# Attention probabilities of 14 of 16 heads turned on VectorE and through DRAM instead of on TensorE

## The chip, the cores and the metric

The kernel runs on 1 core of one Trainium2 chip. The metric is the device time of one execution, in microseconds (us). Engines are named as in the profile: PE is TensorE (PEld its weight loads), DVE is VectorE, ACT is ScalarE, POOL is GpSimd, SP is SyncE, which issues nearly all DMA transfers.

## What is computed

Two layers of a bidirectional encoder over 256 tokens of width 2048, in float32. Each layer projects the normalized input, runs three groups of attention heads side by side, gates them and projects back:

```
for l in range(DEPTH):                                   # 2
    proj = rmsnorm(x, norm_g[l]) @ w_in[l]               # 2048 columns to 5824
    ya = swa_attention(...)     # 8 heads, window |t-s| <= 128, sink logit, ALiBi
    yb = mla_attention(...)     # 4 heads, low-rank q and kv, rotary part
    yc = diff_attention(...)    # 4 heads, two softmax maps: a0 - lam * a1
    y = concat([ya * silu(a_g), yb * silu(b_g), yc * silu(c_g)])
    x = x + y @ w_out[l]
return rmsnorm(x, final_norm)
```

Every head makes a 256 x 256 map of probabilities p[q, k] by softmax over the keys, and then `out = p @ v`.

## The kernel before

All matrix products are done as three (or, stacked, two) products of halves: a float32 value is split into a rounded part `hi` and a rest `lo`, both of the type float32r. Weights come in pieces of 512 KB (line 150, tile `raw`, 4 buffers, issued by SP), are split by ACT into `whi` (line 176) and by DVE into `wlo` (line 177), 3 buffers each, and are used by PE. The list `pieces` sets the order: for each layer the wide projection (line 408), values of the C heads, up-projections of the B heads, gates, q and k of the C heads, then keys, queries and gates of the A heads (line 970 on), and 32 pieces of the output projection (line 834). Per piece of a transposed projection (`proj_t`, line 425) PE does 8 products with `whi` (line 437, 512 columns) and 8 with `wlo` (line 442, 256 columns).

The loop at line 1043 walks the pieces. `ahead` (line 984) puts loads up to four pieces and splits up to two pieces ahead into the program. `clock` counts pieces; `later(n, fn)` puts the work of a head n pieces on. Within an engine the instructions run in the order in which a list scheduler put them; PE follows the written order (`in_order`, line 76). SP issues its transfers in one row too: one that waits holds up all that stand behind it.

A head of group A or B goes like this. `scores` (lines 577 and 607): PE makes S = q k into PSUM, DVE adds the bias, DVE takes the maximum (line 540), ACT the exponential and its sum (line 542), DVE the reciprocal `rr` and the multiplication by it (lines 589 and 617, two halves of 128 x 256). The result is `sb`, queries on partitions, keys along the row. Three pieces later `transpose_p` (line 546): PE turns it in four 128 x 128 transposes into the PSUM tile `PT` (line 550), ACT and DVE split that into `pth` and `ptl` (line 181 and 183, through `halves`). Two pieces after that, `pv` (line 556): six products into `O`, and `put_y` (line 562) gates the result into `yhi`, `ylo`. A head of group C makes two maps one piece apart, `difference` (line 647) scales one on DVE (line 651) and subtracts (line 652), and the transposes follow five pieces after the first scores.

A map thus passes PE, DVE, ACT, DVE, PE, ACT and DVE, and PE again.

Of the kernel before, what the change touches and what calls it, by code (L numbers as in the profile page):

```python
# [61 lines left out]
def trunk(ctx, tc, x, positions, w_in, swa_sink, mla_w_uq, mla_w_ukv, diff_lambda, w_out, final_norm,  # L62
# [4 lines left out]
    const = pool("const")  # L67
    keep = pool("keep")
    wts = pool("wts")
    work = pool("work")  # L70
    small = pool("small", 4)
    acc = pool("acc", 4, space=bass.MemoryType.PSUM)
    att = pool("att", 4, space=bass.MemoryType.PSUM)

# [459 lines left out]
    def softmax(S_ps, sb, w, name):  # L534
# [8 lines left out]
        nc.vector.reciprocal(rr, sm)  # L543
        return rr

    def transpose_p(sb, name):
        ps = att.tile([P, NT, S], F32, tag="att", name=f"PT{name}")
        for kt in range(NT):
            for t in range(NT):
                nc.tensor.transpose(ps[:, kt, t * P:(t + 1) * P], sb[:, t, kt * P:(kt + 1) * P], ident)  # L550
        hi = work.tile([P, NT, S], F32R, tag="pth", bufs=2, name=f"pth{name}")
        lo = work.tile([P, NT, S], F32R, tag="ptl", bufs=2, name=f"ptl{name}")
        halves(hi, lo, ps)
        return hi, lo

    def pv(pt, v, d0, name):
        o = att.tile([P, S], F32, tag="att", name=f"O{name}")
        for kt in range(NT):
            mm3(o, v[0][:, kt, d0:d0 + P], v[1][:, kt, d0:d0 + P], pt[0][:, kt, :], pt[1][:, kt, :], kt == 0, kt == NT - 1)
        return o  # L560

    def put_y(L, e, o, gate):
# [5 lines left out]
        nc.vector.tensor_tensor(lo, y, hi.bitcast(F32), ALU.subtract)  # L568
        L.y[e] = (hi, lo)

    LAG_T, LAG_V = 3, 5

    def head_a(L, h):
        name = f"A{L.l}_{h}"
        st = {}

        def scores():
            ps = att.tile([P, NT, S], F32, tag="att", name=f"S{name}")
            (qh, ql), (kh, kl) = L.qa.pop(h), L.ka[h // (A_HEADS // A_KV)]
            for t in range(NT):  # L580
                ts = slice(t * P, (t + 1) * P)
                mm3(ps[:, t, :], qh[:, ts], ql[:, ts], kh, kl, True, True)
            sb = work.tile([P, NT, S + 1], F32, tag="sb", bufs=3, name=f"sb{name}")
            nc.vector.scalar_tensor_tensor(sb[:, :, :S], dist_a, -(2.0 ** -(h + 1)), ps, ALU.mult, ALU.add)
            i = L.l * A_HEADS + h
            nc.vector.tensor_copy(sb[:, :, S:S + 1], late["sink"][:, i:i + 1].unsqueeze(1).broadcast_to([P, NT, 1]))
            rr = softmax(None, sb, S + 1, name)
            for t in range(NT):
                nc.vector.tensor_scalar(sb[:, t, :S], sb[:, t, :S], rr[:, t:t + 1], None, ALU.mult)
            st["sb"] = sb  # L590

        def trans():
            st["pt"] = transpose_p(st["sb"], name)

        def out_():
            o = pv(st["pt"], L.va, (h // (A_HEADS // A_KV)) * P, name)
            put_y(L, h, o, L.ga.pop(h))

        scores()
        later(LAG_T, trans)  # L600
        later(LAG_V, out_)

    def head_b(L, h):
        name = f"B{L.l}_{h}"
        st = {}

        def scores():
            ps = att.tile([P, NT, S], F32, tag="att", name=f"S{name}")
            (qh, ql), (kh, kl) = L.qb.pop(h), L.kb.pop(h)
            for t in range(NT):  # L610
                ts = slice(t * P, (t + 1) * P)
                mm3(ps[:, t, :], qh[:, ts], ql[:, ts], kh, kl, True, False)
                mm_stacked(ps[:, t, :], L.qr[h // 2][h % 2], L.kr, ts, False, True)
            sb = work.tile([P, NT, S + 1], F32, tag="sb", bufs=3, name=f"sb{name}")
            rr = softmax(ps, sb, S, name)
            for t in range(NT):
                nc.vector.tensor_scalar(sb[:, t, :S], sb[:, t, :S], rr[:, t:t + 1], None, ALU.mult)
            st["sb"] = sb

        def trans():  # L620
            st["pt"] = transpose_p(st["sb"], name)

        def out_():
            o = pv(st["pt"], L.vb, h * P, name)
            put_y(L, A_HEADS + h, o, L.gb.pop(h))

        scores()
        later(LAG_T, trans)
        later(LAG_V, out_)

    def head_c(L, h):
        name = f"C{L.l}_{h}"
        st = {}

        sbs, rrs = [], []
        (q, k) = L.qc.pop(h), L.kc.pop(h)

        def scores(c):
            ps = att.tile([P, NT, S], F32, tag="att", name=f"S{name}_{c}")
            for t in range(NT):  # L640
                mm_stacked(ps[:, t, :], q[c], k[c], slice(t * P, (t + 1) * P), True, True)
            sb = work.tile([P, NT, S + 1], F32, tag="sb", bufs=3, name=f"sb{name}_{c}")
            nc.vector.scalar_tensor_tensor(sb[:, :, :S], dist, -(2.0 ** (-2.0 * (h + 1))), ps, ALU.mult, ALU.add)
            rrs.append(softmax(None, sb, S, f"{name}_{c}"))
            sbs.append(sb)

        def difference():
            lr = small.tile([P, NT], F32, tag="lr", name=f"lr{name}")
            nc.vector.tensor_scalar(lr, rrs[1], lam[:, L.l:L.l + 1], None, ALU.mult)
            for t in range(NT):  # L650
                nc.vector.tensor_scalar(sbs[1][:, t, :S], sbs[1][:, t, :S], lr[:, t:t + 1], None, ALU.mult)
                nc.vector.scalar_tensor_tensor(sbs[0][:, t, :S], sbs[0][:, t, :S], rrs[0][:, t:t + 1], sbs[1][:, t, :S], ALU.mult, ALU.subtract)
            st["sb"] = sbs[0]

        def trans():
            st["pt"] = transpose_p(st["sb"], name)

        def out_():
            o = pv(st["pt"], L.vc, h * P, name)
            sq = work.tile([P, S], F32, tag="ge", bufs=2, name=f"sq{name}")  # L660
            nc.scalar.activation(sq, o, AF.Square)
            hi = work.tile([P, S], F32R, tag="kf", bufs=2, name=f"sqh{name}")
            lo = work.tile([P, S], F32R, tag="kf", bufs=2, name=f"sql{name}")
# [17 lines left out]
        later(LAG_T + 2, trans)  # L681
        later(LAG_V + 3, out_)


    def evac_latent(L, which, t, ps):
        n = QR if which == 0 else KVR
        cn = L.cn[which, t] = work.tile([P, n], F32, tag=("pth", "ptl")[t], bufs=2, name=f"cn{L.l}_{which}_{t}")
# [5 lines left out]
        nc.vector.tensor_scalar(cn, ps[:, :n], rn, None, ALU.mult)  # L693
        if which == 0:
            if t == 0:
                L.krow = small.tile([P, NT, RD], F32, tag="krow", bufs=1, name=f"krow{L.l}")
            nc.vector.tensor_scalar(L.krow[:, t, :], ps[:, QR:QR + RD], r, None, ALU.mult)

    def latent_transpose(L, which):
# [182 lines left out]
    def load_final(L):  # L882
        L.fss = small.tile([P, NT, 5], F32, tag="fss", bufs=1, name="fss")
        L.gf = []
        for j in range(4):
            gf = work.tile([P, 512], F32, tag=("pth", "ptl")[j % 2], bufs=2, name=f"gf{j}")
# [42 lines left out]
    def build(L):  # L929
# [40 lines left out]
        for p in range(4):  # L970
            proj_t(L, w, AQ + 256 * p, lambda f, ps, p=p: evac_qk(L, L.qa, 2 * p + f, ps, P ** -0.5, "q"))
            proj_t(L, w, AG + 256 * p, lambda f, ps, p=p: evac_gate(L, L.ga, 2 * p + f, ps))
            task_piece(lambda p=p: (later(0, lambda: head_a(L, 2 * p)), later(1, lambda: head_a(L, 2 * p + 1))))
        for j in range(4):
            out_chunk(L, j)

# [112 lines left out]
```

## Time and profile before

| | us |
|---|---|
| median of 3 runs (797.11 to 797.41) | 797.26 |
| the profiled execution, whole | 797.44 |
| its span, first to last instruction | 795.1 |
| outside the span | 2.3 |
| PE busy | 785.3 |
| DVE busy | 619.9 |
| ACT busy | 490.1 |

An engine's row says how long it was busy. Matmuls are pipelined, so a PE that is busy throughout need not be at its peak; but when it never waits, each thing taken off it shortens the span. DMA moved 142 MB, and the packets of SP's queue took 58.5% of the time of the 16 DMA engines.

### The profile page before, as it was taken

How to read it: one execution, taken by the hardware profiler on the slowest of the kernel's cores; microseconds unless marked ns; L12 is line 12 of the kernel's file. 1: busy time of each engine (PE TensorE's matmuls, PEld its weight loads, DVE VectorE, ACT ScalarE, POOL GpSimd, SP SyncE). 2: the span in 40 equal slices, each digit the busy share in tenths (PEclk: the TensorE clock that was granted, in tenths of full speed). 3: DMA queues.
4: the chain of work that ended last, by engine and by line, in shares of the span. 5: the costliest groups of instructions: out<-in, count | busy, mean ns of one | idle time of the engine just before them, and what ended most of it. 6: DMA issues, size and time to landing. Idle time of an engine off the chain costs nothing.

```text
span 795.1 us, 12140 instructions
## 1 busy us (share of the span) xinstructions
PE 785.3 (99%) x4384; PEld 687.5 (86%) x4384; DVE 619.9 (78%) x1150; ACT 490.1 (62%) x920; POOL 32.6 (4%) x45
## 2 busy tenths in 40 slices
PE   9999999999999999999999999999999999999995
PEld 8888998888888888888888899988888888888885
DVE  6669997999988798655564878889998987875554
ACT  6668576767776566554454656667776766564442
POOL 4600000000000000000000000000000000002110
PEclk9999999999999999999999999999999999999998
DMA  9965665664665654555556666556565555557652
GB/s 321 364 180 155 185 176 158 161 184 145 172 167 155 169 174 154 165 188 183 189 181 187 179 170 194 147 144 184 142 196 165 158 158 160 164 170 230 198 165 106
DMA packets 113898, 141.99 MB, mean 179 GB/s; under 512 B 8240, under 2 KB 87344, under 8 KB 113840
## 3 DMA queue, kind: packets, MB, share of 16 engines
q1 hardware_dynamic: 113232, 139.69, 58.5%
q0 software_dynamic: 320, 1.05, 0.5%
q8 instruction: 34, 0.56, 0.3%
q10 hardware_dynamic: 288, 0.49, 0.2%
q14 instruction: 24, 0.20, 0.1%
HBM read 139.12 MB, written 2.10 MB: 178 GB/s over the span
## 4 chain that ended last, share of the span: by engine, by line
PE 98%; DVE 1%; DMA 1%; ACT 0%; issue 0%; ACTq 0%; DVEq 0%
PE pt L437 32%; PE pt L442 16%; PE po L386 7%; PE po L387 7%; PE po L389 7%; PE pw L389 4%; PE pw L386 3%; PE pw L387 3%; PE pa L389 2%; PE pa L386 2%; PE pa L387 2%; PE PTA L550 1%; DMA raw<-in_w_wide 1%; PE SA L305 0%; PE SC L496 0%; PE SA L307 0%
## 5 line engine op out<-in xcount | busy, mean ns | idle before, releaser
L177 DVE TENSOR_TENSOR wlo<-raw,whi 128x1024 fp32r<-128x1024 f32 (+1 forms) x257 | 313.5, 1222 | 132.8 <-ACT whi L176 131.2
L176 ACT ACTIVATE whi<-raw 128x1024 fp32r<-128x1024 f32 (+1 forms) x257 | 268.8, 1047 | 169.5 <-PE po L387 57.7
L437 PE MATMUL pt<-h,whi 128*128 128x512 f32 x1088 | 280.5, 395 | 0.0
L437 PEld LDWEIGHTS pt<-h,whi 128*128 128x128 f32 x1088 | 192.8, 188 | 32.5
L442 PEld LDWEIGHTS pt<-h,wlo 128*128 128x128 f32 x1088 | 152.8, 190 | 13.9
L442 PE MATMUL pt<-h,wlo 128*128 128x256 f32 x1088 | 156.9, 282 | 0.0
L386 PE MATMUL po<-whi,yhi 128*128 128x512 f32 (+1 forms) x262 | 101.3, 388 | 0.5 <-DVE x L901 0.5
L387 PE MATMUL po<-whi,ylo 128*128 128x512 f32 (+1 forms) x262 | 100.6, 385 | 0.0
L389 PE MATMUL po<-wlo,yhi 128*128 128x512 f32 (+1 forms) x262 | 70.7, 384 | 0.0
L386 PEld LDWEIGHTS po<-whi,yhi 128*128 128x128 f32 x262 | 49.2, 188 | 10.1 <-DVE x L901 0.7
L387 PEld LDWEIGHTS po<-whi,ylo 128*128 128x128 f32 x262 | 49.2, 188 | 9.4
L389 PEld LDWEIGHTS po<-wlo,yhi 128*128 128x128 f32 x262 | 48.8, 188 | 9.8
L386 PE MATMUL pw<-whi,h 128*128 128x448 f32 (+2 forms) x130 | 49.1, 379 | 0.4 <-ACT whi L168 0.4
L387 PE MATMUL pw<-whi,h 128*128 128x448 f32 (+2 forms) x130 | 48.9, 377 | 0.0
L389 PE MATMUL pw<-wlo,h 128*128 128x448 f32 (+2 forms) x130 | 33.0, 377 | 0.0
L567 ACT ACTIVATE yhi<-y 128x256 fp32r<-128x256 f32 x32 | 13.3, 416 | 30.5 <-DVE y L564 30.5
L887 POOL DMA_DIRECT2D gf<-in_final_norm x4 | 2.4, 598 | 681.1 <-PE OA L307 681.1
L386 PEld LDWEIGHTS pw<-whi,h 128*128 128x128 f32 x130 | 24.5, 188 | 4.2 <-ACT whi L168 0.5
L387 PEld LDWEIGHTS pw<-whi,h 128*128 128x128 f32 x130 | 24.4, 188 | 3.6
L389 PEld LDWEIGHTS pw<-wlo,h 128*128 128x128 f32 x130 | 24.1, 188 | 3.7
L386 PE MATMUL pa<-whi,h 128*128 128x512 f32 x64 | 25.3, 396 | 0.0
L387 PE MATMUL pa<-whi,h 128*128 128x512 f32 x64 | 25.1, 393 | 0.0
(337 smaller groups left out, 1053.2 us busy)
## 6 DMA issues: line engine op xcount, KB each, us to landing
raw<-in_w_in SPq DMA_DIRECT2D x152, 512.0 KB, 3.8
raw<-in_w_out SPq DMA_DIRECT2D x64, 512.0 KB, 4.3
raw<-in_w_wide SPq DMA_DIRECT2D x31, 480.0 KB, 4.0
raw<-in_mla_w_uq SPq DMA_DIRECT2D x18, 128.0 KB, 3.2
x<-in_x SPq DMA_DIRECT2D x4, 512.0 KB, 6.8
raw<-in_mla_w_ukv SPq DMA_DIRECT2D x8, 256.0 KB, 3.6
xt<-in_x_t SPq DMA_DIRECT2D x15, 128.0 KB, 5.4
out<-x SPq DMA_DIRECT2D x2, 768.0 KB, 3.3
```

Source lines behind the costliest of these rows:

```text
L176: nc.scalar.activation(p["hi"], raw, AF.Copy)
L177: nc.vector.tensor_tensor(p["lo"], raw, p["hi"].bitcast(F32), ALU.subtract)
L386: nc.tensor.matmul(ps, lhi, rhi, start=first, stop=False, skip_group_check=part)
L387: nc.tensor.matmul(ps, llo, rhi, start=False, stop=False, skip_group_check=part)
L389: nc.tensor.matmul(ps, lhi, rlo, start=False, stop=last, skip_group_check=part)
L437: nc.tensor.matmul(st["ps"][f], p["hi"][:, kk, f * P:(f + 1) * P], L.hh[k], start=k == 0, stop=False)
L442: nc.tensor.matmul(st["ps"][f][:, S:], p["lo"][:, kk, f * P:(f + 1) * P], L.h[k][0], start=False, stop=k == NK - 1)
L550: nc.tensor.transpose(ps[:, kt, t * P:(t + 1) * P], sb[:, t, kt * P:(kt + 1) * P], ident)
L567: nc.scalar.activation(hi, y, AF.Copy)
L887: nc.gpsimd.dma_start(gf, final_norm[j * 512:(j + 1) * 512].unsqueeze(0).partition_broadcast(P).rearrange("p a c -> p (a c)"))
```

## The change

In 14 of the 16 heads of each layer (all but the A heads 6 and 7, whose flag `by_pe` keeps the old way) PE transposes nothing. Instead:

- `turn_p`: two DVE instructions per head turn `sb` in squares of 32 x 32, 128 x 256 float32 each, directly behind the softmax, into a tile `T` whose row holds, for each of 4 blocks j of keys, all that goes to the partitions of block j: 512 bytes. T lies in the buffers `cTh` and `cTl`, one each, by turns.
- `spill_p`: SP writes T to a DRAM tile (256 KB, 2 KB a partition), two pieces after the softmax was written down; for C heads two pieces after `difference`.
- `fetch_p`: one piece later, SP reads it back in 4 transfers of 64 KB, one for each 32 partitions, in runs of 512 bytes, so that the squares lie in their places, in a tile `R` (tag `ptl`, now 3 buffers).
- `split_p`: three pieces after that ACT makes `hi` from R and DVE leaves R - hi in R itself; both are read from SBUF, where before they were read from PSUM.
- `pv` comes two pieces after that, so eight pieces after the scores where it was five. It reads hi and R in runs of 32 columns, with other runs between them, where it read rows of 256.
- The multiplication by `rr` of the B heads and by `lr` of the C heads goes from DVE to ACT.
- To find room, `small` has 3 buffers in place of 4 and two small tiles (`krow`, `krt`) use other tiles' buffers.

```
+    def turn_p(sb, name):
+        T = work.tile([P, P // Q, NT, NT, Q], F32, tag=("cTh", "cTl")[n_turned[0] % 2], bufs=1, name=f"T{name}")
+        n_turned[0] += 1
+        for t in range(NT):
+            nc.vector.transpose(T[:, :, :, t, :].rearrange("p j k b -> p k j b"),
+                                sb[:, t, :S].rearrange("p (k j b) -> p k j b", k=NT, b=Q))
+        return T
+    def spill_p(T, name):
+        dram = spill.tile([P, P // Q, NT * NT * Q], F32, tag="spill", name=f"D{name}")
+        nc.sync.dma_start(dram, T.rearrange("p j k t b -> p j (k t b)"))
+        return dram
+    def fetch_p(dram, name):
+        R = work.tile([P, P // Q, NT, NT, Q], F32R, tag="ptl", bufs=3, name=f"R{name}")
+        for j in range(P // Q):
+            nc.sync.dma_start(R[j * Q:(j + 1) * Q].rearrange("a i k t b -> a i (k t b)").bitcast(F32),
+                              dram[:, j, :].rearrange("(i a) r -> a i r", a=Q))
+        return R
+    def split_p(R, name):
+        hi = work.tile([P, P // Q, NT, NT, Q], F32R, tag="pth", bufs=2, name=f"hi{name}")
+        halves(hi, R, R.bitcast(F32))
+        return [[x[:, :, kt, :, :].rearrange("p i t b -> p t i b") for kt in range(NT)] for x in (hi, R)]
+    def turn_later(st, name, n, out_, by_pe=False):
+        if by_pe:
+            later(n, lambda: st.update(pt=transpose_p(st["sb"], name)))
+            later(n + 2, out_)
+            return
+        st["T"] = turn_p(st["sb"], name)
+        later(n - 1, lambda: st.update(D=spill_p(st["T"], name)))
+        later(n, lambda: st.update(R=fetch_p(st["D"], name)))
+        later(n + LAG_S, lambda: st.update(pt=split_p(st["R"], name)))
+        later(n + LAG_S + 2, out_)
...
-    LAG_T, LAG_V = 3, 5
+    LAG_T, LAG_S = 3, 3
...
-                nc.vector.tensor_scalar(sb[:, t, :S], sb[:, t, :S], rr[:, t:t + 1], None, ALU.mult)
+                nc.scalar.activation(sb[:, t, :S], sb[:, t, :S], AF.Copy, scale=rr[:, t:t + 1])
...
-                nc.vector.tensor_scalar(sbs[1][:, t, :S], sbs[1][:, t, :S], lr[:, t:t + 1], None, ALU.mult)
+                nc.scalar.activation(sbs[1][:, t, :S], sbs[1][:, t, :S], AF.Copy, scale=lr[:, t:t + 1])
...
-            task_piece(lambda p=p: (later(0, lambda: head_a(L, 2 * p)), later(1, lambda: head_a(L, 2 * p + 1))))
+            task_piece(lambda p=p: (later(0, lambda: head_a(L, 2 * p, p == 3)), later(1, lambda: head_a(L, 2 * p + 1, p == 3))))
```

How the built program stands is shown at three places, before and now. First SP's row at the A heads 4 and 5 of the first layer; `raw104` and so on are pieces, by number. Before:

```order
L153 DMA raw103_3452<-in_w_in 128x4x256
L153 DMA raw104_3483<-in_w_in 128x4x256
L153 DMA raw106_3528<-in_w_out 128x2x512
L153 DMA raw107_3565<-in_w_out 128x2x512
L153 DMA raw108_3600<-in_w_out 128x2x512
```

Now, with T, D and R the tiles named above:

```order
L154 DMA raw103_3510<-in_w_in 128x4x256
L572 DMA DA0_4_3508<-TA0_4_3424 128x512
L154 DMA raw104_3539<-in_w_in 128x4x256
L578 DMA RA0_4_3532<-DA0_4_3508 32x4x128 x4
L572 DMA DA0_5_3537<-TA0_5_3483 128x512
L154 DMA raw106_3580<-in_w_out 128x2x512
L154 DMA raw107_3604<-in_w_out 128x2x512
L578 DMA RA0_5_3575<-DA0_5_3537 32x4x128 x4
L154 DMA raw108_3629<-in_w_out 128x2x512
```

Two transfers of spill and eight of fetch stand among the loads; the loads of pieces 106 and 108 stand behind all of one head's each.

Second, ACT's row at the same heads. Before (`pthA0_5` is the first half of head 5's transposed map):

```order
L181 ACTIVATE q0_6h_3497<-qf0_6_3499 128x256
L460 COPY qf0_7_3513<-pt0_768_1_3394 128x256
L181 ACTIVATE pthA0_5_3524<-PTA0_5_3519 128x512
L176 ACTIVATE whi104_3567<-raw104_3483 128x1024
L181 ACTIVATE q0_6h_3497<-qf0_7_3513 128x256
L567 ACTIVATE yhi0_4_3561<-y0_4_3559 128x256
L176 ACTIVATE whi106_3602<-raw106_3528 128x1024
L567 ACTIVATE yhi0_5_3596<-y0_5_3594 128x256
L176 ACTIVATE whi107_3624<-raw107_3565 128x1024
```

Now:

```order
L182 ACTIVATE q0_6h_3553<-qf0_6_3555 128x256
L177 ACTIVATE whi104_3606<-raw104_3539 128x1024
L182 ACTIVATE q0_6h_3553<-qf0_7_3569 128x256
L182 ACTIVATE hiA0_4_3626<-RA0_4_3532 128x512
L177 ACTIVATE whi106_3631<-raw106_3580 128x1024
L177 ACTIVATE whi107_3656<-raw107_3604 128x1024
L461 COPY g0_6_3668<-pt0_2304_0_3586 128x256
L182 ACTIVATE hiA0_5_3651<-RA0_5_3575 128x512
```

The half of head 4's map stands ahead of the split of piece 106, that of head 5 behind the split of piece 107.

Third, DVE's row at the `difference` of the first C head. Before:

```order
L177 TENSOR_TENSOR wlo57_1915<-raw57_1846,whi57_1914 128x1024
L543 RECIPROCAL rrC0_0_1_1879<-smC0_0_1_1878 128x2
L649 TENSOR_SCALAR lrC0_0_1906<-rrC0_0_1_1879,lam_99 128x2
L651 TENSOR_SCALAR sbC0_0_1_1875<-sbC0_0_1_1875,lrC0_0_1906 128x256 x2
L652 SCALAR_TENSOR_TENSOR sbC0_0_0_1837<-sbC0_0_0_1837,rrC0_0_0_1841,sbC0_0_1_1875 128x256 x2
L177 TENSOR_TENSOR wlo58_1937<-raw58_1884,whi58_1936 128x1024
L461 TENSOR_TENSOR cqf0_2_1948<-pt0_4032_0_1852,cqf0_2_1948 128x256
```

Now (`STREAM_TRANSPOSE` is the turn in squares):

```order
L178 TENSOR_TENSOR wlo57_1936<-raw57_1864,whi57_1935 128x1024
L544 RECIPROCAL rrC0_0_1_1897<-smC0_0_1_1896 128x2
L684 TENSOR_SCALAR lrC0_0_1924<-rrC0_0_1_1897,lam_101 128x2
L178 TENSOR_TENSOR wlo58_1958<-raw58_1902,whi58_1957 128x1024
L687 SCALAR_TENSOR_TENSOR sbC0_0_0_1855<-sbC0_0_0_1855,rrC0_0_0_1859,sbC0_0_1_1893 128x256 x2
L566 STREAM_TRANSPOSE TC0_0_1930<-sbC0_0_0_1855 128x2x4x32 x2
L462 TENSOR_TENSOR cqf0_2_1969<-pt0_4032_0_1870,cqf0_2_1969 128x256
```

The two multiplications by `lr` are gone, the split of piece 58 has moved up into their place, and two turns stand behind the subtraction.

## Rows read from the trace of the kernel before

**Rows 1.** The page, parts 1 and 4: engines, chain by engine.

```profile
PE 785.3 (99%) x4384; PEld 687.5 (86%) x4384; DVE 619.9 (78%) x1150; ACT 490.1 (62%) x920; POOL 32.6 (4%) x45
...
PE 98%; DVE 1%; DMA 1%; ACT 0%; issue 0%; ACTq 0%; DVEq 0%
```

**Rows 2.** Who waited for whom, PE, the whole span.

```profile
PE warm L110 <- DVE still L106: 1.2, 1, 1.2
PE po L386 <- DVE x L901: 0.5, 1, 0.5
PE pw L386 <- ACT whi L168: 0.4, 1, 0.4
```

**Rows 3.** Timeline of PE, A heads 4, 5 and 6 (start us, us, instructions).

```profile
286.98 0.60 PE L550 MATMUL PTA<-ident,sbA 128*128 128x128 f32 x4
287.33 1.17 PE L437 MATMUL pt<-h,whi 128*128 128x512 f32 x4
288.35 0.64 PE L442 MATMUL pt<-h,wlo 128*128 128x256 f32 x4
288.82 1.09 PE L437 MATMUL pt<-h,whi 128*128 128x512 f32 x4
289.75 0.64 PE L442 MATMUL pt<-h,wlo 128*128 128x256 f32 x4
...
293.46 0.28 PE L305 MATMUL OA<-pthA,vah 128*128 128x256 f32 x1
...
294.17 1.99 PE L437 MATMUL pt<-h,whi 128*128 128x512 f32 x8
...
303.23 0.28 PE L305 MATMUL SA<-k_0h,q_6h 128*128 128x256 f32 x1
...
303.94 0.40 PE L386 MATMUL po<-whi,yhi 128*128 128x512 f32 x1
```

**Rows 4.** PE group of the A heads' transposes (busy us, mean ns | idle before).

```profile
L550 PE MATMUL PTA<-ident,sbA 128*128 128x128 f32 x64 | 9.6, 272 | 0.0
```

**Rows 5.** DVE groups by shape, columns as in the group above.

```profile
L462 DVE TENSOR_TENSOR g<-g,R 128x256 f32<-128x256 f32 x32 | 13.4, 420 | 0.5
...
L589 DVE TENSOR_SCALAR sbA<-sbA,rrA 128x256 f32<-128x256 f32 x32 | 9.8, 349 | 0.1
L364 DVE SCALAR_TENSOR_TENSOR h<-xt,gcol,h 128x256 fp32r<-128x256 f32 x15 | 7.8, 521 | 0.9 <-ACT h L363 0.9
...
L651 DVE TENSOR_SCALAR sbC<-sbC,lrC 128x256 f32<-128x256 f32 x16 | 4.9, 350 | 0.2
```

**Rows 6.** ACT group by shape, columns as above.

```profile
L567 ACT ACTIVATE yhi<-y 128x256 fp32r<-128x256 f32 x32 | 13.3, 416 | 30.5 <-DVE y L564 30.5
```

**Rows 7.** DMA issues (count, KB each, median us from issue to landing).

```profile
raw<-in_w_out SPq DMA_DIRECT2D x64, 512.0 KB, 4.3
...
x<-in_x SPq DMA_DIRECT2D x4, 512.0 KB, 6.8
...
out<-x SPq DMA_DIRECT2D x2, 256.0 KB, 2.3
```

**Rows 8.** Transfers of line 818: issue on SP in ns, min/median/max; landing.

```profile
L818 SPq DMA_DIRECT2D raw<-in_mla_w_uq x18: 367/466/1172, 55.5 to 465.3; - x18
...
DMA to landing us min/median/max: 2.2/3.3/5.5
```

**Rows 9.** One stretch: PE, PEld, DVE, ACT, POOL busy, PEclk, DMA share, GB/s.

```profile
160.00:240.00 80.00, 80.00 (x489) 71.44 (x489) 74.09 (x145) 58.73 (x124) 0.00 (x0) 1.00 0.59 168
```

**Rows 10.** Timeline of SP: the first loads for the output projection.

```profile
286.97 11.98 SPq L153 DMA_DIRECT2D raw<-in_w_out  x5
```

**Rows 11.** Timeline of DVE: the A heads 4 and 5 are scaled.

```profile
285.17 0.61 DVE L589 TENSOR_SCALAR sbA<-sbA,rrA 128x256 f32<-128x256 f32 x2
...
287.02 0.62 DVE L589 TENSOR_SCALAR sbA<-sbA,rrA 128x256 f32<-128x256 f32 x2
```

**Rows 12.** Timeline of ACT: the first piece of the output projection is split.

```profile
296.24 1.06 ACT L176 ACTIVATE whi<-raw 128x1024 fp32r<-128x1024 f32 x1
```

More of the change, by code (lines that the diff above doesn't have):

```diff
@@ L69, in trunk @@
     wts = pool("wts")
+    spill = pool("spill", 4, space=bass.MemoryType.DRAM)
     work = pool("work")
-    small = pool("small", 4)
+    small = pool("small", 3)
     acc = pool("acc", 4, space=bass.MemoryType.PSUM)
@@ L551, in transpose_p @@
         hi = work.tile([P, NT, S], F32R, tag="pth", bufs=2, name=f"pth{name}")
-        lo = work.tile([P, NT, S], F32R, tag="ptl", bufs=2, name=f"ptl{name}")
+        lo = work.tile([P, NT, S], F32R, tag="ptl", bufs=3, name=f"ptl{name}")
         halves(hi, lo, ps)
-        return hi, lo
+        return [[x[:, kt, :] for kt in range(NT)] for x in (hi, lo)]
+    Q = 32
+    n_turned = [0]
+    def turn_p(sb, name):
[29 more added lines that the diff above has]
+        later(n + LAG_S + 2, out_)
     def pv(pt, v, d0, name):
@@ L558, in pv @@
         for kt in range(NT):
-            mm3(o, v[0][:, kt, d0:d0 + P], v[1][:, kt, d0:d0 + P], pt[0][:, kt, :], pt[1][:, kt, :], kt == 0, kt == NT - 1)
+            mm3(o, v[0][:, kt, d0:d0 + P], v[1][:, kt, d0:d0 + P], pt[0][kt], pt[1][kt], kt == 0, kt == NT - 1)
         return o
@@ L569, in put_y, with head_a @@
         L.y[e] = (hi, lo)
-    LAG_T, LAG_V = 3, 5
-    def head_a(L, h):
+    LAG_T, LAG_S = 3, 3
+    def head_a(L, h, by_pe):
         name = f"A{L.l}_{h}"
@@ L590, in scores @@
             st["sb"] = sb
-        def trans():
-            st["pt"] = transpose_p(st["sb"], name)
         def out_():
@@ L599, in head_a @@
         scores()
-        later(LAG_T, trans)
-        later(LAG_V, out_)
+        turn_later(st, name, LAG_T, out_, by_pe)
     def head_b(L, h):
@@ L616, in scores @@
             for t in range(NT):
-                nc.vector.tensor_scalar(sb[:, t, :S], sb[:, t, :S], rr[:, t:t + 1], None, ALU.mult)
+                nc.scalar.activation(sb[:, t, :S], sb[:, t, :S], AF.Copy, scale=rr[:, t:t + 1])
             st["sb"] = sb
-        def trans():
-            st["pt"] = transpose_p(st["sb"], name)
         def out_():
@@ L627, in head_b @@
         scores()
-        later(LAG_T, trans)
-        later(LAG_V, out_)
+        turn_later(st, name, LAG_T, out_)
     def head_c(L, h):
@@ L650, in difference @@
             for t in range(NT):
-                nc.vector.tensor_scalar(sbs[1][:, t, :S], sbs[1][:, t, :S], lr[:, t:t + 1], None, ALU.mult)
+                nc.scalar.activation(sbs[1][:, t, :S], sbs[1][:, t, :S], AF.Copy, scale=lr[:, t:t + 1])
                 nc.vector.scalar_tensor_tensor(sbs[0][:, t, :S], sbs[0][:, t, :S], rrs[0][:, t:t + 1], sbs[1][:, t, :S], ALU.mult, ALU.subtract)
             st["sb"] = sbs[0]
-        def trans():
-            st["pt"] = transpose_p(st["sb"], name)
+            turn_later(st, name, LAG_T, out_)
         def out_():
@@ L680, in head_c @@
         later(2, difference, nc.vector)
-        later(LAG_T + 2, trans)
-        later(LAG_V + 3, out_)
     def evac_latent(L, which, t, ps):
         n = QR if which == 0 else KVR
-        cn = L.cn[which, t] = work.tile([P, n], F32, tag=("pth", "ptl")[t], bufs=2, name=f"cn{L.l}_{which}_{t}")
+        cn = L.cn[which, t] = work.tile([P, n], F32, tag=("pth", "ptl")[t], bufs=2 + t, name=f"cn{L.l}_{which}_{t}")
         r = L.r[:, t:t + 1]
@@ L695, in evac_latent @@
             if t == 0:
-                L.krow = small.tile([P, NT, RD], F32, tag="krow", bufs=1, name=f"krow{L.l}")
+                L.krow = work.tile([P, NT, RD], F32, tag="ge", bufs=2, name=f"krow{L.l}")
             nc.vector.tensor_scalar(L.krow[:, t, :], ps[:, QR:QR + RD], r, None, ALU.mult)
@@ L727, in key_rope @@
     def key_rope(L):
-        kt = small.tile([P, NT, 2, RD], F32, tag="krt", bufs=1, name=f"krt{L.l}")
+        kt = work.tile([P, NT, 2, RD], F32, tag="y32", bufs=1, name=f"krt{L.l}")
         tmp = work.tile([P, NT, 1, RD], F32, tag="lo64", bufs=4, name=f"krtmp{L.l}")
@@ L885, in load_final @@
         for j in range(4):
-            gf = work.tile([P, 512], F32, tag=("pth", "ptl")[j % 2], bufs=2, name=f"gf{j}")
+            gf = work.tile([P, 512], F32, tag=("pth", "ptl")[j % 2], bufs=2 + j % 2, name=f"gf{j}")
             nc.gpsimd.dma_start(gf, final_norm[j * 512:(j + 1) * 512].unsqueeze(0).partition_broadcast(P).rearrange("p a c -> p (a c)"))
```

## The prediction

> **What bounds the kernel now.** I read the page first. PE is busy 785.3 of 795.1 us, and the chain that ended last runs over PE for 98% of the span [rows 1]. A busy PE alone proves little, so the list of waits came next: PE waited three times, 2.1 us in all, twice at the start and once for the last add [rows 2]. Nothing that DVE, ACT or SP does for the heads is ever waited for. So the time is the sum of what PE issues, and a stretch is worth what lies between the starts of its neighbours in PE's timeline, not the durations, which overlap.
>
> **What the change takes from PE.** Four transposes of the A head 4 start at 286.98, the product behind them at 287.33: 0.35 us. That product is the first of four which last until 288.35, 1.02 us; the next four, with no transpose ahead, take 288.82 to 289.75, 0.93 us [rows 3]. So 0.09 us of a switch goes too, and a head gives back 0.44 us. There are 14 heads in each of 2 layers: 28 x 0.44 = 12.3 us. Without the switch it would be 28 x 0.35 = 9.8; the group's busy time gives more, 9.6 us for 64 or 0.15 each, 16.8 for 112 [rows 4], but that counts overlap with the neighbours and can't come back whole. I take 12.3, with 9.8 as the lower end and 12.6 (0.45 a head, the rounding of the rows) as the upper.
>
> The Trainium skill, "VectorE: DVE Perf Modes", The three transpose paths, gives 390 ns for a 128 x 128 transpose on TensorE (bf16) and 311 ns on VectorE, and its Rules for kernel authors send such a transpose to TensorE where PSUM will do as its destination, which speaks against this change. By 390 ns each the 112 would be worth 43.7 us and the kernel would take about 753.8; the trace disagrees, since the starts lie 0.09 us apart.
>
> **What it adds to PE.** The six products of `pv` stay, 293.46 to 294.17, 0.12 us each [rows 3], but read the map in runs of 32 columns. No row shows such a read. Its price lies between nothing and, as the far end, twice the interval, 168 x 0.12 = 20.2 us. I take nothing: the amount of data is the same and a run is long. The far end is a rival below.
>
> **What it adds to DVE.** No row shows a turn in squares. The nearest is one pass over 128 x 256 float32 from SBUF, 0.42 us; the ends are the quick multiplication, 0.35, and the slowest row of that size, 0.52 [rows 5]. 56 turns make 23.5 us (19.6 to 29.1). The B and C heads lose 32 multiplications of 0.35, 11.2 us. DVE gets 12.3 us more (8.4 to 17.9) on 619.9, which is 632 of a span of 783, 81%. The split of R costs what that of PT cost. POOL gets nothing.
>
> **What it adds to ACT.** The 32 multiplications, at 0.42 us from the nearest row [rows 6], 13.4 us on 490. For a C head they stand between two DVE steps, but the order shows that DVE does the split of piece 58 meanwhile, 1.2 us of work that stood behind them; so DVE finds them done. In both engines this lies beside PE's work and costs nothing as long as the splits of weights stay ahead.
>
> **What it adds to SP's queue.** A spill waits for DVE's turns, a fetch for the spill's landing, and loads of weights stand behind both. I walk the A heads 4 and 5, the tightest place. Their scaling ends at 285.78 and 287.64 [rows 11]; with turns of 0.42, T4 is there at 286.6 and T5, behind T4's turns too, at 289.3. The nearest landing for a spill is a store of 256 KB, 2.3 us; the loads of line 818, 128 and 256 KB, land after 3.3 in the median and 5.5 at most [rows 7, 8]. With 3.3, D4 has landed at 289.9. An issue takes 0.47 us [rows 8], the four fetches 1.9: 291.8. D5 is issued by 292.3 and the load of piece 106 at 292.3. Before it was issued at 286.97 [rows 10], split by ACT at 296.24 [rows 12], and used at 303.94 [rows 3]. Now it lands at 292.3 + 4.3 [rows 7] = 296.6 and is split by ACT and DVE by about 299, some 5 us before PE wants it. The map's way: R4 lands around 295.1 (297.3 at 5.5); ACT's half stands just ahead of the split of piece 106, so that split waits for it, and has the same 5 us. `pv` moves three pieces back, to about 303.2 [rows 3], 4 us or more after R4 is split. All of this is cover, so the sum has nothing for it; without the cover each pair of heads would pay the excess.
>
> The bytes are 28 x 512 KB, 14.7 MB on 142, and the DMA share in the stretches of the heads is 0.59 [rows 9]; I leave landing times as they are. The fewer `small` buffers and the moved small tiles touch only work that nothing waits for.
>
> **The sum.** The profiled execution took 797.44 us (span 795.1, 2.3 around it), 0.18 over the median of the runs. 797.44 - 12.3 = 785.1; against the median 784.9. I predict **785.0**. The terms' ends, 12.6 and 9.8, make 784.7 to 787.6.
>
> **The rivals.**
> A, the way through DRAM is too slow (slower). SP's wait for a spill is the mechanism, the A pairs the place. It decides from 5 us over my walk. If a spill took the 6.8 us of the slowest median [rows 7] and an issue the 1.17 us of the slowest one [rows 8], the load of piece 106 would come 3.5 + 5 x 0.7 = 7 us later: PE would wait 2 us, and the same again behind the pair's second fetch, 4 us for each of 6 A pairs, and as much for the 2 sets of B heads. 8 x 4 = 32 us less 12.3 gives about 817; break-even is 1.5 us a pair. Against it: loads of twice the size land in 4.3 us, and the queue has room. For it: no row shows a read right behind its own write.
> B, `pv` reads its runs slowly (slower). From 12.3 / 168 = 73 ns a product it eats the gain; at twice the interval the time is 785.1 + 20.2 = 805. Nothing here shows it. The Trainium skill, "Advanced Engine Details and Errata", SBUF Cachelines, says that accesses to the same 16-byte line run at full rate; a run here is 128 bytes, so by it the price is nothing, and no run here shows that yet.
> C, DVE becomes the bound where the C heads run (still faster). It is busy 74.1 of 80 us there [rows 9]. Three C heads add 6 x 0.07 = 0.4 us and the first two A heads 4 x 0.42 = 1.7, so 76.2, while PE's 80 shrink by six heads to 77.4. If the 5.9 us in which DVE idles there (it waits for ACT's halves) could not shrink, it would need 82.1; 4.7 us over, less some 2 us of lead that the splits have, is 2.7 a layer, 5.4 in all: 790.5, and without any lead 794.5. For it: 98% busy. Against it: the idle time is waiting for splits that themselves wait for PE to free a buffer, and shrinks as PE moves on.
> D, no change: PE's freed time is eaten by small waits that add up to the gain, 797. That needs 0.44 us a head everywhere, where now there is none.
>
> **How the numbers follow.** Forecast 0.60, C 0.18, A 0.09, B 0.06, D 0.07. A measurement of this kernel can tell about 0.2% from no change, 1.6 us. Faster is the forecast and C, 0.78; same is D, 0.07; slower is A and B, 0.15. The range goes from 783.5, a little under the sum's end since a modelled PE end may hide small waits that go with the transposes, to 792, which takes in C with most of its ends; it leaves out A, B and D.
>
> **What would show it.** Right: transposes of line 550's kind only for the heads 6 and 7, PE busy some 12 us less, PE still without waits, DVE near 630 us, turns of 0.35 to 0.52 us. Step by step: the walk is right if the load of piece 106 is issued around 292 and no product waits for `whi`, `wlo`, `hi` or R. Wrong: waits of PE on `wlo` in the C stretch (C), on `whi` or `hi` behind SP's waits (A), or `pv` products more than 0.12 us apart (B).

## The result and the profile after

The changed kernel takes 786.22 us in the median (785.18 to 786.74) against 797.34 before (797.11 to 797.82): 0.9856 of it, with a 95% interval of 0.9844 to 0.9869, 11.1 us less. Measured once more beside other versions it took 785.66 (785.09 to 786.32) against 797.47, a ratio of 0.9853 [0.984, 0.9865]. The prediction was 785.0, with 783.5 to 792: right in its sign and in its range, 0.7 to 1.2 us too low.

The profiled execution took 786.74 us, its span 785.0. The first part of its page, and the chain, answer to [rows 1]:

```profile
PE 773.9 (99%) x4272; PEld 675.5 (86%) x4272; DVE 626.1 (80%) x1174; ACT 500.2 (64%) x952; POOL 33.0 (4%) x45
...
PE 97%; DVE 1%; DMA 1%; ACT 0%; issue 0%; SPq 0%; DVEq 0%
```

PE has 112 instructions and 11.4 us less, DVE 6.2 and ACT 10.1 us more, and PE is still the bound. The list of its waits, to be laid beside [rows 2], has one new wait, the last; the one on `whi` at the start is there in both, 0.4 and 0.6 us:

```profile
PE warm L111 <- DVE still L107: 1.2, 1, 1.2
PE pw L387 <- ACT whi L177: 0.6, 1, 0.6
PE po L387 <- DVE rf_t L297: 0.5, 1, 0.5
PE pt L443 <- DVE wlo L178: 0.4, 1, 0.4
```

What the time of PE's stream did can be read between two events that both kernels have: the first product of a B head's scores, which comes before any transpose, and the first product behind PE's wait for the last adds. Of the kernel before, the first view is the tile SB on PE (after the durations, first and last start), the second PE's timeline:

```profile
L305 PE MATMUL SB<-kb_0h,qb_0h x8: 278/278/279, 94.6 to 494.0; 128*128 128x256 f32 x8
```

```profile
784.94 0.39 PE L386 MATMUL po<-whi,yhi 128*128 128x256 f32 x1 [0.51 <-DVE x L901]
```

The same two views of the changed kernel:

```profile
L306 PE MATMUL SB<-kb_0h,qb_0h x8: 278/278/279, 95.1 to 489.1; 128*128 128x256 f32 x8
```

```profile
774.11 0.38 PE L387 MATMUL po<-whi,yhi 128*128 128x256 f32 x1 [0.51 <-DVE rf_t L297]
```

From 94.6 to 784.94 are 690.3 us, from 95.1 to 774.11 are 679.0: 11.3 less. I call this the stretch of the heads; it leaves out the start, whose length varies, and the tail. The first event is read to 0.1 us, so a difference holds to about 0.1. The same two events in the profiles of the versions below:

| version | first SB, last add (us) | stretch | against before | median time |
|---|---|---|---|---|
| before | 94.6, 784.94 | 690.3 | 0 | 797.3 |
| the change | 95.1, 774.11 | 679.0 | -11.3 | 786.2 |
| the change again | 94.1, 772.47 | 678.4 | -12.0 | 785.7 |
| all heads by PE | 95.0, 787.02 | 692.0 | +1.7 | 799.1 |
| only A heads by DRAM | 94.8, 781.88 | 687.1 | -3.3 | 794.7 |
| only B and C by DRAM | 94.7, 778.04 | 683.3 | -7.0 | 790.8 |
| before, map in runs | 95.1, 785.93 | 690.8 | +0.5 | 797.8 |
| fetch in 8 | 94.8, 777.51 | 682.7 | -7.6 | 790.4 |
| fetches on POOL's queue | 94.6, 812.33 | 717.7 | +27.4 | 823.2 |
| pv at six pieces | 94.8, 775.72 | 680.9 | -9.4 | 788.6 |
| pv at seven pieces | 94.3, 773.66 | 679.4 | -11.0 | 787.4 |
| without the way | 95.1, 773.55 | 678.5 | -11.9 | 785.8 |
| scaling on DVE | 94.7, 773.11 | 678.4 | -11.9 | 785.8 |
| all 16 heads | 95.1, 772.64 | 677.5 | -12.8 | 784.6 |

### The profile page after: what moved, and what is told of

Same layout as the page of the kernel before. It is cut to its first block, busy times and chain, and to the rows that moved or that the text cites. A ratio compares the mean times of both kernels' runs of the same rounds, so it can differ in the third digit from the quotient of the medians.

```text
span 785.0 us, 12295 instructions
## 1 busy us (share of the span) xinstructions
PE 773.9 (99%) x4272; PEld 675.5 (86%) x4272; DVE 626.1 (80%) x1174; ACT 500.2 (64%) x952; POOL 33.0 (4%) x45
## 3 DMA queue, kind: packets, MB, share of 16 engines
q0 software_dynamic: 320, 1.05, 0.5%
## 4 chain that ended last, share of the span: by engine, by line
PE 97%; DVE 1%; DMA 1%; ACT 0%; issue 0%; SPq 0%; DVEq 0%
PE pt L438 32%; PE pt L443 16%; PE po L387 7%; PE po L388 7%; PE po L390 7%; PE pw L387 3%; PE pw L390 3%; PE pw L388 3%; PE pa L387 2%; PE pa L390 2%; PE pa L388 2%; DMA raw<-in_w_wide 1%; PE SC L496 0%; PE OA L307 0%; PE SA L306 0%; PE SC L497 0%
## 5 line engine op out<-in xcount | busy, mean ns | idle before, releaser
L387 PEld LDWEIGHTS po<-whi,yhi 128*128 128x128 f32 x262 | 49.2, 188 | 10.1 <-DVE x L932 0.7
```

What stands on the lines that cost most here:

```text
L387: nc.tensor.matmul(ps, lhi, rhi, start=first, stop=False, skip_group_check=part)
```

## The experiments

**All heads by PE again**, the rest of the change kept (`by_pe` true everywhere):

```diff
-    turn_later(st, name, LAG_T, out_)          # B and C
+    turn_later(st, name, LAG_T, out_, True)
...
-    head_a(L, 2 * p, p == 3)                   # and the second of the pair
+    head_a(L, 2 * p, True)
```

> All heads are transposed on PE again and pv comes five pieces after the scores; the rest of the change stays (scaling of B and C heads on ACT, buffers). Theory 1, the gain is PE's own: the 112 transposes come back at 0.42 us a head (in the new trace PE gains 11.7 us on 28 heads beside one wait of 0.4), so 797.3 us within 0.5, and PE waits 2.1 us as before. Rival: part of the gain comes from the moves that stay here (32 multiplications less on DVE, 11.2 us by the prediction): then 786 to 795. Rival on the other side: the moves cost something that the new way hid, over 798.5.

799.06 us (798.56 to 799.62), ratio 1.002 [1.0011, 1.0029]: 1.6 us more than before, the rival on the other side. Its list of PE's waits shows the place:

```profile
PE OC L307 <- DVE ptlC L184: 1.0, 2, 0.5
```

This version differs from the kernel before in one thing more than the scaling on ACT and the buffers. In the kernel before, `pv` of a C head comes eight pieces after its first scores (its own line adds three to `LAG_V`), in the change ten (the eight that stand ahead of the prediction hold for the A and B heads); with `by_pe` it comes at seven. In both layers that is too early for one C head. Its transposes run at 180.26 and ACT's half is done at 181.85, but DVE has eight subtractions of another head's keys and a gate to do before it comes to `ptlC`, and PE can use that only at 187.78, after a wait of 0.50 us (DVE):

```profile
183.23 3.44 DVE L492 TENSOR_TENSOR ckl<-ckf,ckh 64x256 fp32r<-64x256 f32 x8
186.71 0.42 DVE L607 TENSOR_TENSOR y<-OC,rsC 128x256 f32<-128x256 f32 x1
187.05 0.68 DVE L184 TENSOR_TENSOR ptlC<-PTC,pthC 128x512 fp32r<-128x512 f32 x1
```

In the kernel before, `pv` of that head starts 9.6 us after its transposes, here 6.0. So without the way through DRAM nothing is gained, and what is kept costs 1.6; the rows put it on the shorter lag and DVE's order. Whether the scaling on ACT has a share was not tested apart from the lag. In the change the wait is gone.

**Only the A heads, and only the B and C heads, through DRAM** (one of the two edits above each).

> Only the 12 A heads (0 to 5 of both layers) go through DRAM; the 16 heads of B and C are transposed on PE. Theory 1 with PE's own price: 12 x 0.41 = 4.9 us less, and the one wait of PE on wlo (0.4 us in the first layer, the place where the A heads 2 and 3 lie) stays, so 797.3 - 4.9 + 0.4 = 792.8. Rival, the late landings around the A pairs come from the traffic of the B and C heads too: then the wait goes and it is 792.4 or less. Rival, A heads give nothing: 797.

> Only the 16 heads of B and C go through DRAM; the A heads are transposed on PE. Theory 1: 16 x 0.43 = 6.9 us less and no wait of PE on wlo, so 790.4. If gains add, this and the version with A heads alone together give the whole change: 4.5 + 6.9 = 11.4 against 11.1 measured. Rival C of the prediction (DVE bounds the stretch of the C heads) would leave 793 or more, with waits of PE on wlo there.

794.66 us (794.44 to 795.06), ratio 0.9966 [0.9954, 0.9979], and 790.75 (790.25 to 790.97), ratio 0.9915 [0.9901, 0.9928]. Neither has a wait of PE on `wlo`. The first is 1.9 over its 792.8: it still has the C heads at seven pieces and the two waits on `ptlC`, so it is to be laid beside the 799.06, 4.4 us for 12 heads. The second is 6.7 below before, 0.42 a head, where 6.9 was expected. Laid beside 799.06 it is 8.3, and 4.4 + 8.3 = 12.7 against 12.8 for the whole change (13.4 by its second measurement): the groups add. By stretches it is 692.0 - 687.1 = 4.9 and 692.0 - 683.3 = 8.7, together 13.6, and 692.0 - 678.4 is 13.6. Without the C heads' 1.6 us: B and C give 690.3 - 683.3 = 7.0 for 16 heads, 0.44 each; the A heads the rest, 683.3 - 678.4 = 4.9 for 12, 0.41 each.

**The map in runs, on the kernel before**: PE transposes, the split writes the layout of the change.

```diff
-        halves(hi, lo, ps)
-        return hi, lo
+        row = lambda x: x.rearrange("p i k t b -> p (k t) i b")
+        halves(row(hi), row(lo), ps.rearrange("p k (t i b) -> p (k t) i b", t=NT, i=4))
+        return [[x[:, :, kt, :, :].rearrange("p i t b -> p t i b") for kt in range(NT)] for x in (hi, lo)]
```

> The kernel before, whose split writes the map in the layout of the change, so that pv reads it in runs of 32 columns; PE still transposes, nothing goes through DRAM. 168 products with such reads. Theory: the read costs nothing, 797.3 us, products of pv 0.28 us each as in both kernels. Rival B of the prediction: twice the interval, 0.12 us for each of 168, 817 us; at its break-even of 73 ns, 809.6. If the writes of ACT and DVE in runs get longer, that lies beside PE's work and shows in their rows alone.

797.79 us (797.45 to 798.43), ratio 1.0005 [0.9996, 1.0015]: no change. A product of `pv` takes 0.28 us in the median, as before. Rival B falls.

**The change again, beside three versions of it.**

> The changed kernel itself, unaltered, beside the next three: 786.2 us within 0.5. If its one wait of PE on wlo (0.4 us, at 258.5 in the first layer) hangs on the chance of landing times, it may be gone or stand elsewhere in this profile; if it hangs on the order of DVE's work, it stands at the same place with the same size.

785.66 us. In this profile the wait on `wlo` is gone; PE's list has only the two waits that every version has:

```profile
PE warm L111 <- DVE still L107: 1.2, 1, 1.2
PE po L387 <- DVE rf_t L297: 0.5, 1, 0.5
```

So the wait of 0.4 us comes and goes from run to run. But DVE's order is the same in both, and it leaves hardly a margin. In the first profile ACT had the `whi` of that piece early (first fence, ACT), DVE came to its `wlo` only behind the softmax and the turn of A head 2 (second fence, DVE), and PE stood waiting (third, PE):

```profile
250.50 1.04 ACT L177 ACTIVATE whi<-raw 128x1024 fp32r<-128x1024 f32 x1
```

```profile
255.12 0.43 DVE L611 TENSOR_TENSOR ylo<-y,yhi 128x256 fp32r<-128x256 f32 x1
255.46 0.62 DVE L632 TENSOR_SCALAR sbA<-sbA,rrA 128x256 f32<-128x256 f32 x2
255.99 0.77 DVE L566 STREAM_TRANSPOSE TA<-sbA 128x256 f32<-128x256 f32 x2
256.68 0.65 DVE L541 TENSOR_REDUCE nmA<-sbA 128x2 f32<-128x514 f32 x1
257.24 2.35 DVE L178 TENSOR_TENSOR wlo<-raw,whi 128x1024 fp32r<-128x1024 f32 x2
```

```profile
258.51 0.74 PE L443 MATMUL pt<-h,wlo 128*128 128x256 f32 x4 [0.35 <-DVE wlo L178]
```

The half was ready to be taken at 251.5 and taken at 257.2: 5.7 us of the lead went on DVE's order. The row `ylo` in between belongs to head 1; `pv` of the heads 0 and 1 at eight pieces falls on the scores of the next pair.

What uses up the last of the margin is a transfer. A little earlier ACT waits for a piece of weights, in the first profile and in the second:

```profile
243.93 1.06 ACT L177 ACTIVATE whi<-raw 128x1024 fp32r<-128x1024 f32 x1 [2.28 <-DMA raw<-in_w_in]
```

```profile
242.14 1.06 ACT L177 ACTIVATE whi<-raw 128x1024 fp32r<-128x1024 f32 x1 [1.53 <-DMA raw<-in_w_in]
```

ACT's and PE's work ahead of it lies 1.05 us apart in the two profiles, this split 1.79, and DVE keeps that distance up to the `wlo` (257.24 against 255.46). So the load came 0.7 us later in the first, and PE's 0.35 us are what was left of that. In the kernel before, and in the version without the way below, ACT waits for no load at this place; why the load came later in one run is not shown.

**A fetch in 8 transfers**, to hold SP longer:

```diff
         for j in range(P // Q):
-            nc.sync.dma_start(R[j * Q:(j + 1) * Q] ..., dram[:, j, :] ...)
+            for e in range(2):
+                nc.sync.dma_start(R[j * Q:(j + 1) * Q, 2 * e:2 * e + 2] ...,
+                                  dram[e * 2 * Q:(e + 1) * 2 * Q, j, :] ...)
```

> Every fetch goes in 8 transfers of 32 KB in place of 4 of 64 KB, the same bytes: 4 more issues of SP for each head, at 0.42 us 1.7 us a head and 3.4 for an A pair, which hold back the loads behind them. Theory 1, the walk on record (some 5 us of cover behind SP's queue): no more waits than before, 786.2. Rival, the cover is already used up (in the new trace the split of piece 91's wlo ends 0.1 us after PE wants it, and the lead from landing to split has shrunk from 4 to 6 us to 0.1 at the A pairs): the excess comes through, 3.4 us less some 1 us of lead for each of 6 A pairs, 14 us, so 800.

790.37 us (789.28 to 790.76), ratio 0.9909 [0.9895, 0.9923]: 4.7 us more than the change, between the two expectations. PE waits on the map:

```profile
PE OA L306 <- ACT hiA L182: 1.5, 2, 0.9
...
PE OA L307 <- DMA raw<-in_w_in: 1.2, 2, 0.6
```

Each of the two lines has 2 waits, one in each layer, at `pv` of A head 3, 2.7 us in all. (The product of the second line reads RA; the releaser there is inferred.) So the cover lay below the 3.4 us that this adds to a pair, but at one pair in each layer, not at all six.

**The fetches on POOL's queue.**

```diff
-            nc.sync.dma_start(R[j * Q:(j + 1) * Q] ...
+            nc.gpsimd.dma_start(R[j * Q:(j + 1) * Q] ...
```

> The four transfers of a fetch are issued by POOL's queue instead of SP's; the spills stay on SP. It takes 1.8 us for each head off SP's queue, so the loads of weights behind them are issued earlier. Theory SP (loads are late because SP's queue holds them back; load of piece 89 lands 7.7 us after its issue): landing comes earlier, the wait of PE on wlo goes, 785.6 us. Theory DVE (the wait comes from DVE's order, where put_y of one A pair, the scores of the next and its turn stand ahead of a split): the wait stays, 786.2. Rival on the other side: POOL's transfers land later than SP's 4.1 us; PE then waits on hi or R of a head, and the time is over 786.8.

823.24 us (820.51 to 828.14), ratio 1.033 [1.0305, 1.0356]. PE's waits are those of rival A:

```profile
PE pt L443 <- DVE wlo L178: 8.3, 8, 2.7
PE PTA L553 <- ACT whi L177: 5.0, 2, 2.8
PE OC L307 <- DVE RC L184: 4.8, 2, 3.1
PE pt L438 <- ACT whi L177: 3.0, 2, 2.7
```

And ACT's timeline shows how a late map reaches the weights: `hiC` waits for its fetch, and the `whi` behind it waits too.

```profile
213.23 0.63 ACT L182 ACTIVATE hiC<-RC 128x512 fp32r<-128x512 f32 x1 [5.16 <-DMA RC<-DC]
...
214.69 1.04 ACT L177 ACTIVATE whi<-raw 128x1024 fp32r<-128x1024 f32 x1
```

An issue on POOL takes 0.55 us instead of 0.42, and the fetches land 4.8 us after it for the A heads and 4.0 for the C heads, instead of 4.1 and 3.2; that does not explain 37.6 us by itself. The delay grows on the way: the turn of this head comes on DVE at 201.4 instead of 196.3, its spill on SP at 202.2 instead of 197.1, its fetch lands late, ACT stops, and the turn of the next head is 7.9 us later than in the change where this one is 5.1. What set it off, the issues, the later landings or the moved order around them, was not separated. It does show that a way through DRAM that is too slow costs about as much as rival A said, here by another queue than the one that A named.

**`pv` of the A heads at six and at seven pieces**: the split of R two pieces after the fetch, `pv` one or two pieces after the split.

```diff
-        later(n + LAG_S, lambda: st.update(pt=split_p(st["R"], name)))
-        later(n + LAG_S + 2, out_)
+        later(n + s, lambda: st.update(pt=split_p(st["R"], name)))   # A heads: s = 2
+        later(n + s + o, out_)                                       # o = 1, or 2; B and C: s = 3, o = 2
```

> pv of the A heads 0 to 5 comes six pieces after the scores instead of eight (split two pieces after the fetch, pv one after the split); A pairs follow each other at eight pieces, so with eight put_y of one pair falls on the scores of the next. Theory DVE (that burst makes the split of wlo late): the split moves ahead of the second A head's maximum on DVE, the wait of PE on wlo (0.4) goes, and the time is 785.6 to 785.8. Theory SP (late landings): the wait stays, 786.2. Rival: R lands too late for the earlier split (SP's wait for a turn, up to 7.3 us, moves with it): PE waits on hi or R, over 787.

> pv of the A heads 0 to 5 seven pieces after the scores (split two pieces after the fetch, pv two after the split). It tells apart why the version with pv at six lost 3.0 us without any wait of PE: there single products of pv stand among the wide ones, since the order put the hi and the lo part apart, and each such break costs 0.1 us. Here the six products stand in a row again. Theory order: 785.7 within 0.5. Rival, the loss comes from pv no longer standing next to the scores of the next pair: half of the heads lose that here, 787.2.

788.62 us (788.36 to 789.08), ratio 0.989 [0.9877, 0.9903], and 787.36 (786.29 to 787.9), ratio 0.9877 [0.9861, 0.9894], and PE has no wait in either beyond the two that remain, so none of the three expectations for the first holds: the wait on `wlo` is gone, R comes in time, and yet time is lost. PE's timeline of the first shows the loss, `pv` of A head 2:

```profile
266.40 0.39 PE L306 MATMUL OA<-hiA,vah 128*128 128x256 f32 x1
266.63 1.09 PE L438 MATMUL pt<-h,whi 128*128 128x512 f32 x4
267.55 0.28 PE L443 MATMUL pt<-h,wlo 128*128 128x256 f32 x1
267.74 0.39 PE L307 MATMUL OA<-RA,vah 128*128 128x256 f32 x1
267.96 0.28 PE L308 MATMUL OA<-hiA,val 128*128 128x256 f32 x1
```

The product with `hi` stands alone ahead of four wide ones, the rest behind them. From 266.40 to 266.63 are 0.23 us where a product of 256 columns in its row takes 0.12, from 267.74 to 267.96 0.22. What stands ahead of the prediction says that PE follows the written order; it does within one task, but the scheduler may put pieces of a projection between the products of `pv` where `hi` comes earlier than R. All 12 heads are pulled apart so, once each, and the stretch is 2.5 us longer than that of the change measured beside it, 0.21 each. In the version with seven pieces head 1 is still pulled apart in both layers, and the first products of head 5 stand 0.19 and 0.23 us apart in both, with nothing recorded between them; its stretch is 1.0 longer than the change's, where a clean row should have cost nothing. The products of head 2, which stand in a row there but no longer beside scores, take their 0.12 us each, so what the profile shows of the loss is the broken order and not the missing neighbour, though the time is the rival's. Its median lies another microsecond above its profiled run, which no row explains; that stays open. Whether a shorter lag would free DVE's crowded place could not be read from these two.

**The change without the way**: no turn, no spill, no fetch. The split reads the softmax's own tile, so this version leaves the transposition of these 28 maps out altogether; the split comes three pieces earlier, `pv` where it was.

```diff
-        st["T"] = turn_p(st["sb"], name)
-        later(n - 1, lambda: st.update(D=spill_p(st["T"], name)))
-        later(n, lambda: st.update(R=fetch_p(st["D"], name)))
-        later(n + LAG_S, lambda: st.update(pt=split_p(st["R"], name)))
+        later(n, lambda: st.update(pt=split_p(st["sb"], name)))
```

> The changed kernel without the way: no turn on DVE, no spill, no fetch; the split takes its input from the softmax's own tile, so the maps of 14 heads aren't transposed at all (that part of the computation is left out). All else stays, pv at eight pieces too. It tells what the way itself still costs. Theory 1, PE's return of 0.44 a head is all there is and the way lies beside it: within 0.6 us of the changed kernel (785.7 beside the last three), 785.1 to 785.9. Rival: landing times and the used-up cover cost PE 1 to 2 us in all, then 783.7 to 784.7.

785.83 us (785.71 to 785.9), ratio 0.9856 [0.9841, 0.987], its stretch 678.5 against 678.4 and 679.0 of the change. Taking the way out gains nothing: turns, spills, fetches and 14.7 MB lie beside PE's work, apart from a wait of about half a microsecond that one of two profiles has.

**The scaling of B and C back on DVE.**

```diff
-                nc.scalar.activation(sb[:, t, :S], sb[:, t, :S], AF.Copy, scale=rr[:, t:t + 1])
+                nc.vector.tensor_scalar(sb[:, t, :S], sb[:, t, :S], rr[:, t:t + 1], None, ALU.mult)
```

> The changed kernel with the 32 multiplications of the B and C heads back on DVE (9.9 us on DVE more, 14.5 on ACT less). Rival C of the prediction says that DVE bounds the stretch of the C heads: DVE is busy 75.9 of 80 us there, and 2.5 us a layer more would show as waits of PE on wlo, 5 us in all: 790.7. Theory: DVE's idle time there is only waiting for ACT's halves and shrinks, so no wait: 785.7 within 0.6.

785.8 us (785.7 to 786.22), ratio 0.9856 [0.9842, 0.9871], with DVE busy 632.4 us and no new wait among the heads. Rival C falls: DVE has room for still more in that stretch. ACT's part of the change is worth nothing.

**All 16 heads**, the last pair with shorter lags:

```diff
+        n, s, o = (2, 2, 1) if last else (n, LAG_S, 2)
```

> The heads 6 and 7 go through DRAM too, with shorter lags (spill one, fetch two, split four, pv five pieces after the scores), so that their result is there for the eighth piece of the output projection. Theory: four more heads at 0.42 us, 1.7 less, and products of pv that stand alone between wider ones on PE (a lone one takes 0.23 us instead of 0.12) give back 0.4: 784.4. Rival: the way of head 7 is too long for the eighth piece, PE waits some 3 us in each layer: 790.

784.59 us (784.33 to 785.12), ratio 0.9841 [0.9826, 0.9856]. No wait of PE is added, and the stretch is 0.9 shorter than the change's, less than the 1.3 expected: `pv` of the heads 6 and 7 is pulled apart too. This version is the fastest of all in the median; against the change it is 1.1 to 1.6 us less, and the two intervals overlap.

## Why the prediction came out right, step by step

**What PE gives back.** The mechanism held. Where four transposes stood ahead of four products [rows 3], the changed kernel's timeline has the products alone:

```profile
281.95 1.11 PE L443 MATMUL pt<-h,wlo 128*128 128x256 f32 x8
282.90 1.09 PE L438 MATMUL pt<-h,whi 128*128 128x512 f32 x4
283.83 0.63 PE L443 MATMUL pt<-h,wlo 128*128 128x256 f32 x4
```

282.90 to 283.83 is 0.93 us, not 1.02: the switch is gone too. The term was 28 x 0.44 = 12.3 us; the stretch gave 11.9 to 12.0 without the wait, 0.425 a head. B and C heads gave the 0.44, A heads 0.41, so the term was 0.3 to 0.4 too large. It lies well above the end without the switch, 9.8, and far from the group's busy time [rows 4]. An estimate by the Trainium skill's 390 ns for a 128 x 128 transpose ("VectorE: DVE Perf Modes", The three transpose paths) makes the 112 worth 43.7 us; here 12.0 / 112 is 0.107 us. The same page of the Trainium skill (Rules for kernel authors) leaves such a transpose to TensorE where PSUM will do as its destination; in this kernel, where PE is the bound and the other engines have room, taking 112 of them off TensorE made it 11.1 us faster.

**From PE's stream to the time.** The other half of the miss is in what the sum held constant. The profiled run before and the second one of the change differ by 797.44 - 785.09 = 12.35 us: 12.0 in the stretch, 0.5 at the start (94.6 against 94.1), 0.5 less outside the span (2.3 against 1.8), and 0.7 lost between the last add and the end (10.2 against 10.8 us). In the first profile it is 11.3, with the start 0.5 the other way: 10.7. That the second lands on the sum's 785.1 is therefore luck: without its early start it would be 785.6. The start moves between 94.1 and 95.1 us over these profiles; PE's waits on `whi` there, none to 0.7 us, go with it only in part, since two of the starts at 95.1 have none. A longer tail and a shorter rest outside show wherever heads go through DRAM; the version without the way has 10.2 and 2.1. No instruction shows there, and the net is 0.2 us.

**DVE.** The turns took 0.42 us, and they stand in the groups (columns as in [rows 4]):

```profile
L566 DVE STREAM_TRANSPOSE TA<-sbA 128x256 f32<-128x256 f32 x24 | 9.2, 420 | 0.0
...
L566 DVE STREAM_TRANSPOSE TB<-sbB 128x256 f32<-128x256 f32 x16 | 6.5, 431 | 0.2
...
L566 DVE STREAM_TRANSPOSE TC<-sbC 128x256 f32<-128x256 f32 x16 | 6.1, 419 | 0.0
```

Together 21.8 us busy for the 23.5 predicted, since two follow each other in 0.77; the multiplications that left had been busy 9.9, not 11.2. By groups that makes 11.9, near the 12.3 of the sum. The page's total rose by only 6.2: it counts a time in which two instructions overlap once, while all rows of DVE, count times mean, add up to 11.6 us more. That more instructions stand back to back in the crowded stretches would explain it; this last is argued, not shown. "Near 630" was 626.

**ACT.** The multiplications took 0.50 us, not the 0.42 of [rows 6]; 14.5 us busy, not 13.4:

```profile
L656 ACT ACTIVATE sbB<-sbB,rrB 128x256 f32<-128x256 f32 x16 | 7.3, 502 | 0.1
L686 ACT ACTIVATE sbC<-sbC,lrC 128x256 f32<-128x256 f32 x16 | 7.2, 501 | 0.0
```

In the change it costs nothing (785.8 with the scaling back on DVE).

**The walk of SP's queue.** For the pair that it walks it held. SP's timeline and ACT's (compare [rows 10] and [rows 12]):

```profile
286.77 0.34 SPq L572 DMA_DIRECT2D DA<-TA  x1
287.21 0.94 SPq L154 DMA_DIRECT2D raw<-in_w_out  x2
289.17 1.76 SPq L578 DMA_DIRECT2D RA<-DA  x4
```

```profile
291.96 1.06 ACT L177 ACTIVATE whi<-raw 128x1024 fp32r<-128x1024 f32 x1 [2.02 <-DMA raw<-in_w_out]
```

PE uses the piece at 298.3 here, so the load of piece 106 is issued 11.1 us ahead; the walk had 303.94 - 292.3 = 11.6. (The "around 292" of the prediction's signs did not allow for the 5.6 us that PE has gained by then; the time is 287.21.) ACT and DVE have split it some 4 us ahead of PE, the walk said 5. The issues (count, KB each, median us to landing) answer to [rows 7, 8]:

```profile
raw<-in_w_out SPq DMA_DIRECT2D x64, 512.0 KB, 4.5
DA<-TA SPq DMA_DIRECT2D x12, 256.0 KB, 2.3
RA<-DA SPq DMA_DIRECT2D x48, 64.0 KB, 4.1
```

A spill of the A heads lands in 2.3 us, not 3.3, and a read right behind its own write in 4.1. What the walk missed is the place: it took the heads 4 and 5 for the tightest and SP for the engine. The tightest are the heads 2 and 3 (there the transfers in 8 parts and the first profile waited), and the lead there goes on DVE's order as much as in SP's queue, whose late load took the last of it. The step that failed is "the tightest place"; its cost was half a microsecond.

**The rivals.** A did not happen, but its margin was thinner than 5 us: 3.4 us more on SP for a pair brought 4.7 in all, and without them a load came late enough in one run for PE to wait 0.35. B: no price. The trace agrees with the sentence of the Trainium skill that was laid beside it ("Advanced Engine Details and Errata", SBUF Cachelines): runs of 128 bytes are read at the old rate. C: DVE is busy 75.87 of 80 us in the stretch of [rows 9] and PE busy throughout:

```profile
160.00:240.00 80.00, 80.00 (x481) 71.26 (x480) 75.87 (x150) 60.13 (x129) 0.00 (x0) 1.00 0.69 200
```

The idle time of DVE shrank, as the argument against C had it. D did not happen.

## What to carry to other kernels

Where one engine is the bound, price what leaves it by the distance of its neighbours' starts, group by group, and not by its busy time: that gave 0.44 us a head against a measured 0.425. Then look for the cover at every place where the pattern repeats, and on each engine's order as well as in the queue; the tightest place may be the one where two lags fall on each other. And compare single executions between events inside the stretch that was changed: start and tail moved by as much as the prediction missed.

## What was not expected

- The start varies by a microsecond between two profiles of the same kernel (first scores at 94.1 and 95.1 us), which is most of the 1.65 us between them (785.09 and 786.74).
- A shorter lag can cost time without any wait: a product of 256 columns that stands alone among products of 512 takes 0.23 us instead of 0.12, and 12 heads with such breaks lost 2.5 us of the stretch.
- Four transfers for each head on POOL's queue instead of SP's made the kernel 37.6 us slower, though POOL is busy only 33 us in all in the change.
- One piece less of lag cost 1.6 us: with `pv` of the C heads at seven pieces after the first scores, PE waits for `ptlC` in each layer and the products are pulled apart; at eight, in the kernel before, and at ten, in the change, it does not. (The scaling on ACT was kept too; the two were not separated.)
